# 64 unused bytes behind every operand tile of the fp32r products in a macaron decoder layer

## The chip, the cores and the metric

The kernel runs on one core of one Trainium2 chip. The metric is the device time of one execution in microseconds; the median of three runs of the kernel before is 2115.93 us (2115.43 to 2119.53).

## The reference

One decoder layer on 256 tokens of width 2048, in float32: two SwiGLU feed forwards (width 5632) around a mixer, each behind a norm that a conditioning vector modulates.

```python
mod = (silu(c) @ w_ada + b_ada).reshape(B, 9, D)          # sh, sc, ga of three sublayers
h = rms_norm(x, pre_g) * (1 + sc1) + sh1
x = x + 0.5 * ga1 * rms_norm(swiglu(h, w_gate, w_up, w_down), post_g)
h = rms_norm(x, mix_pre_g) * (1 + sc2) + sh2
x = x + ga2 * rms_norm(hybrid_mixer(h, w_in, w_out, ...), mix_post_g)
h = rms_norm(x, ffn2_pre_g) * (1 + sc3) + sh3
x = x + 0.5 * ga3 * rms_norm(swiglu(h, w_gate2, w_up2, w_down2), post_g2)
```

`swiglu` is `(silu(h @ w_gate) * (h @ w_up)) @ w_down`. The mixer projects h with `w_in`, runs a gated delta rule on eight heads and causal attention on eight, and projects with `w_out`. About 510 MB of weights are read once.

## The kernel before

Each weight is loaded as float32 in pieces of 512 KB (`raw`, line 109) and split into two fp32r parts, `whi` by ScalarE (line 99) and `wlo` by VectorE (line 100). The activations are split in the same way: h into `hh`/`hl`, the product of gate and up into `ghi`/`glo`, the mixer's output into `yth`/`ytl`. A product of two split operands is three matmuls into the same PSUM bank (`prod`, lines 118 to 123): hi by hi, hi by lo, lo by hi.

Three kinds of such products exist. In the feed forwards' gate and up products and in most of the mixer's projections the stationary operand is 128 columns of h and the moving one 512 columns of a weight (1664 triples). In the down products and those with `w_out` the stationary operand is 128 columns of `ghi`/`glo` or `yth`/`ytl`, the moving one again 512 columns of a weight (704 and 128 triples). In the convolved projections (`conv_unit`) the weight is stationary and 256 columns of h move (384 triples). For every matmul TensorE loads 128 new stationary columns (PEld in the profile), and it does so while the matmul before it streams. The order of work is the order of the code; all tiles are placed by pools, tag by tag, and a tag with n buffers has n places.

Where the operand tiles lie follows from their sizes. Every operand tile takes 4096 bytes of a partition, as does `raw`; four places of `raw`, four of `whi`, four of `wlo` and the eight tiles of h stand behind each other, so that all of them have the same offset within 4096 bytes (2496). Behind them stand the small tiles of the pool `sm`, and behind these the places of `ghi`/`glo` or `yth`/`ytl`, each at offset 2560 within 4096 bytes, 64 bytes further than those of h and the weights. The slices that a matmul reads lie at multiples of 512 bytes in their tile. So in every product with h the stationary slice begins at the same offset within 512 bytes as the moving one, and in every product with `ghi`, `glo`, `yth` or `ytl` 64 bytes behind it.

In the list below, a helper of two matmuls for the gates of the mixer (lines 683 and 685) also matters: stationary are 32 or 16 columns of a tile `ab`, moving are 256 columns of h.

Of the kernel before, what the change touches and what calls it, by code (L numbers as in the profile page):

```python
# [17 lines left out]
P = 128  # L18
# [5 lines left out]
PARTS = (range(0, 4), range(4, 8), range(8, NF))  # the blocks of a feed forward's three down products  # L24
# [6 lines left out]
LEAD = 14  # units of the first feed forward that advance together while h comes  # L31
STEPS = ((0, 2), (2, 5), (5, 8), (8, 12), (12, 16))  # the k chunks of h that come together
FIRST = 2  # pieces of w_ada loaded ahead of x
DRAIN, EARLY = 2, 1  # units before a step's end at which its modulation and the next h are made
FILL1, FILL2, FILL3 = 0.52, 0.78, 0.2  # pieces of w_ada per piece of weights
RB, WB = 4, 4
NB4, NB2 = 7, 12
WARM = 18  # products that bridge a norm
APART = 2  # k chunks of a first unit done one token tile at a time
# stages between an instruction on the vector engine and the product that takes its result  # L40
# [35 lines left out]
class Layer:  # L76
# [6 lines left out]
    def step(self):  # L83
        """Moves the work that runs beside the weight products on by one stage."""
        for q in self.queues:
            while q:
                if next(q[0], True):
                    q.pop(0)
                    continue
                break  # L90
# [5 lines left out]
    # ---------------------------------------------------------------- weights  # L96
    def split(self, src, hi, lo):
        """src = hi + lo exactly, in two fp32r parts."""
        self.nc.scalar.copy(hi, src)  # L99
        self.nc.vector.tensor_tensor(lo, src, hi.bitcast(F32), op=ALU.subtract)  # L100

    def wtile(self, src):
        """A [rows, cols] tile of weights, split; returns the parts of its k-th 128 rows."""
        rows, cols = src.shape
        n, h = rows // P, 1024 // cols
        out = []
        for k in range(0, n, h):
            m = min(h, n - k)
            t = self.rawp.tile([P, h, cols], F32, name="raw", tag="raw")[:, :m]
            self.nc.sync.dma_start(t, src[k * P:(k + m) * P].rearrange("(c p) n -> p c n", p=P))  # L110
            hi = self.wp.tile([P, h, cols], F32R, name="whi", tag="whi")[:, :m]
            lo = self.wp.tile([P, h, cols], F32R, name="wlo", tag="wlo")[:, :m]
            self.split(t, hi, lo)
            out.append((hi, lo))
            self.fill()
        return lambda c: (out[c // h][0][:, c % h], out[c // h][1][:, c % h])

    def prod(self, out, a, b, first, last):
        """out += (a0+a1)^T (b0+b1) without a1^T b1, which lies below float32."""
        mm = self.nc.tensor.matmul  # L120
        mm(out, a[0], b[0], start=first, stop=False)  # L121
        mm(out, a[0], b[1], start=False, stop=False)  # L122
        return mm(out, a[1], b[0], start=False, stop=last)  # L123

    def unit(self, acc, rows, src, col, stat, pair=False):
        """acc[tok, 512] = stat^T W[:, col:col+512] over the parts rows of W, four k chunks each.

        With pair, one token tile is done with the last two parts before the other begins them.
        """
        rows = list(rows)  # L130
        groups = [[r] for r in rows[:-2]] + ([rows[-2:]] if pair else [[r] for r in rows[-2:]])
        for g in groups:
            ws = [self.wtile(src[r * 512:(r + 1) * 512, col:col + 512]) for r in g]
            for t in range(NT):
                s = slice(t * P, (t + 1) * P)
                for r, w in zip(g, ws):
                    for c in range(4):
                        hi, lo = stat(r * 4 + c)
                        self.mm = self.prod(acc[t], (hi[:, s], lo[:, s]), w(c), r == rows[0] and c == 0,
                                            r == rows[-1] and c == 3)  # L140
                self.step()

    def bank(self, kind, shape):
        """A PSUM bank for weight products ("acc") or for all else; the tags take turns."""
# [12 lines left out]
    # ---------------------------------------------------------------- modulation  # L157
# [7 lines left out]
    def after(self, eng):  # L165
        """Keeps the first modulation work of an engine behind the norm of the step before."""
# [7 lines left out]
    def ada_step(self, acc, srcs, k):  # L174
        """acc += silu(c)[rows] * rows for the 128-row chunks k.. of some column blocks."""
# [14 lines left out]
    def ada_jobs(self, v, done):  # L190
        """The jobs that stream column block v of w_ada, half a megabyte each."""
# [22 lines left out]
    def fin_shift(self, i, js, acc):  # L214
        """sh of sublayer i for the k chunks js, laid over partitions."""
# [7 lines left out]
    def fin_scale(self, i, js, acc):  # L223
        """g * (1 + sc) of sublayer i."""
# [10 lines left out]
    def fin_gate(self, i, js, acc):  # L235
        """ga * post_g of the mixer, laid over partitions."""
# [9 lines left out]
    def fin_gate_rows(self, i, js, acc):  # L246
        """0.5 * ga * post_g of a feed forward sublayer for the k chunks js, on all partitions."""
# [14 lines left out]
    def gate_rows(self, i, n):  # L262
        """Block n of the gate of sublayer i, on all partitions."""
# [21 lines left out]
    # ---------------------------------------------------------------- norms  # L285
    def rsqrt(self, out, t, tag):
        """out = t ** -0.5 for t > 0: a guess from the bits, then Newton steps to float32.

        With r = a s, a step is s <- (t a^2 s^2 - 3) s and a <- -a / 2; a goes -8, 4, -2, 1.
        """  # L290
# [10 lines left out]
    def rsqrt1(self, out, t, tag):  # L301
        """rsqrt of one value per partition, which can then be a scalar operand.

        With r = a s, a step is s <- (q t s^2 - 3 q / a^2) s and a <- -a^3 / (2 q); a goes 1, -1/2, 1/16, 1.
        """
# [10 lines left out]
    def rstd(self, parts, n, tag):  # L316
        """(sum / n + eps) ** -0.5 from the partial sums parts[P, NT, m]."""
# [7 lines left out]
    def new_h(self):  # L325
        self.hT = [[self.hp.tile([P, 4, SEQ], F32R, name=f"h{p}{g}", tag=f"h{p}{g}") for p in "hl"]
                   for g in range(4)]

    def diag(self, dg, t, s, eng=None):
        """dg[:, t] = diag(s[:, t])."""  # L330
# [4 lines left out]
    def warm(self):  # L335
        """Keeps the tensor engine's clock up while it waits for a norm."""
# [6 lines left out]
    def make_h(self, i, terms, ks, ts=range(NT)):  # L343
        """hT of the k chunks ks; the normalised input is the sum of dg[:, t] src(t, k) over terms,
        or src(t, k) itself.

        Returns the last ScalarE and VectorE instructions.
        """
# [27 lines left out]
    def stats(self):  # L376
        """Partial sums [stat, NT, block] of y^2, 2 x * G y, (G y)^2 and x^2."""
# [8 lines left out]
    def y_block(self, n, t, y, src, st, G, nxt):  # L386
        """y = G * src for block n of one token tile, with its sums."""
# [12 lines left out]
    def finish(self, i, ys, st, first=None):  # L400
        """x += rstd(y) * y; then the next sublayer's h and its first unit, columns col.. of src, or the result."""
# [31 lines left out]
        for t in range(NT):  # L433
# [6 lines left out]
            # mean of (x + r G y)^2  # L440
# [64 lines left out]
    # ---------------------------------------------------------------- feed forward  # L505
    def ffn(self, i, wg, wu, wd, start=None, first=None):
# [5 lines left out]
        def product(u, acc, place=None):  # L512
            """silu(g) * u of a block, in place or in a tile of its own."""
# [10 lines left out]
        def turn(n):  # L524
            """A block of products, transposed and split."""
# [8 lines left out]
            hi = self.gp.tile([P, 4, SEQ], F32R, name="ghi", tag="ghi")  # L534
            lo = self.gp.tile([P, 4, SEQ], F32R, name="glo", tag="glo")
# [43 lines left out]
    def lead(self, units, src, start, product, turn):  # L579
        """The first units, k chunk by k chunk as h comes; all but two gather in SBUF."""  # L580
# [43 lines left out]
    # ---------------------------------------------------------------- mixer  # L624
    def tok_unit(self, col):
        """acc[tok, 512] of w_in's columns col.. ."""
# [4 lines left out]
    def conv_unit(self, which, half):  # L631
        """silu(conv(h W)) of four heads of q, k or v, as [channel, head, tok]."""
# [19 lines left out]
    def norm_sums(self, t, ss):  # L652
        """ss = sums of squares over the channels, [tok, NT, head], plus eps."""
# [13 lines left out]
    def gates(self):  # L667
        """beta, the log decay g and its sums over each chunk."""
# [34 lines left out]
        # softplus(t) = max(t, 0) + log1p(exp(-|t|)), log1p(e) = 2 artanh(e / (2 + e))  # L703
# [26 lines left out]
    def z_unit(self, half, z, acc=None):  # L730
        """z[half] = silu(h W_z) * norm_g."""
# [6 lines left out]
    def gdn(self, half, qT, kT, vT, ssq, ssk, o):  # L738
        """The gated delta rule of four heads, in two chunks of 128 tokens."""
# [46 lines left out]
        for u in range(NT):  # L786
# [4 lines left out]
            # T = ((I + L)^-1)^T by doubling the size of the inverted diagonal blocks  # L791
# [42 lines left out]
        # rms_norm(rq * o) without its gain  # L834
# [19 lines left out]
    def gdn_gate(self, half, o, z):  # L854
        """o * z, transposed and split."""
# [13 lines left out]
    def rope_unit(self, col, name):  # L869
        """Four heads of q or k with the rotary turn, as [channel, head, tok]."""  # L870
# [18 lines left out]
    def moba(self, half, raw, V):  # L889
        """Causal attention inside the one block of 256 tokens."""  # L890
# [66 lines left out]
    def mixer(self, acc):  # L957
        nc = self.nc
        self.yT = [[self.yp.tile([P, 4, SEQ], F32R, name=f"yt{p}{g}") for p in "hl"] for g in range(4)]
# [47 lines left out]
    # ---------------------------------------------------------------- whole layer  # L1007
# [91 lines left out]
    def plan(self, vs, rate):  # L1099
        """Column blocks of w_ada to stream beside the weights, rate pieces per piece."""  # L1100
# [33 lines left out]
```

## Time and profile before

| what | value |
|---|---|
| median of three runs | 2115.93 us |
| span of the profiled execution (its own time is not given beside it) | 2121.1 us |
| TensorE (PE) busy | 2064.7 us, 97% |
| weight loads (PEld) busy | 1724.1 us, 81% |
| VectorE (DVE) busy | 1506.6 us, 71% |
| ScalarE (ACT) busy | 957.4 us, 45% |
| mean DMA rate | 243 GB/s |

The profiled execution's span is 5.2 us above the median of the runs, so it is told of in its own times. In the profile a matmul's duration holds the way through the array, and its end is modelled; matmuls overlap. What a matmul costs TensorE in a row of equal ones is read from the distance between the starts of successive matmuls, which is shorter than the duration of one.

### The profile page before, as it was taken

The numbers are of one execution on the slowest core, as the hardware profiler recorded it, in microseconds if no ns is written. First come the engines' busy times: TensorE is split into PE (matmuls) and PEld (weight loads), VectorE is DVE, ScalarE is ACT, GpSimd is POOL, SyncE is SP. The second block draws the span as 40 slices with busy tenths as digits, with TensorE's granted clock in tenths as the row PEclk, the third lists the DMA queues.
The fourth block names the chain that finished last, engine by engine and source line by source line (L and its number), as shares of the span: only waits on it lengthen the run. The fifth ranks groups of instructions, "written<-read, shape, count | busy, mean of one in ns | idle before, by whom it ended". The sixth has DMA issues, their size and how long they took to land.

```text
span 2121.1 us, 27412 instructions
## 1 busy us (share of the span) xinstructions
PE 2064.7 (97%) x10234; PEld 1724.1 (81%) x10234; DVE 1506.6 (71%) x2001; ACT 957.4 (45%) x1212; POOL 8.5 (0%) x13
## 2 busy tenths in 40 slices
PE   4999999999999999999999999999999999999997
PEld 3777788877888777999988888778887888788886
DVE  6889898767667588897887887785446644545455
ACT  4544354443334356554344364544444444334443
POOL 0000000000000000000000000000000000000001
PEclk9999999999999999999999999999999999999999
DMA  9899987878788786987775777587657866566654
GB/s 309 295 301 308 320 291 244 297 258 311 247 296 290 233 288 188 288 254 232 248 229 181 240 237 267 167 289 241 195 182 254 270 188 190 189 189 188 193 184 138
DMA packets 279509, 514.84 MB, mean 243 GB/s; under 512 B 17536, under 2 KB 79248, under 8 KB 279120
## 3 DMA queue, kind: packets, MB, share of 16 engines
q1 hardware_dynamic: 279088, 512.02, 75.0%
q8 instruction: 80, 1.31, 0.3%
q0 software_dynamic: 288, 1.07, 0.2%
q14 instruction: 53, 0.43, 0.1%
HBM read 510.93 MB, written 2.10 MB: 242 GB/s over the span
## 4 chain that ended last, share of the span: by engine, by line
PE 81%; DMA 9%; DVE 6%; issue 2%; ACT 1%; SPq 1%; DVEq 0%; ACTq 0%
PE acc L121 24%; PE acc L122 24%; PE acc L123 24%; DMA ada<-w_ada 8%; DVE wlo L100 3%; PE ms L755 3%; DVE acc L188 2%; PE ms L207 1%; PE ms L532 1%; DMA G<-gr 1%; PE ms L761 1%; ACT whi L99 0%; DMA raw<-w1g 0%; PE ms L360 0%; PE ms L662 0%
## 5 line engine op out<-in xcount | busy, mean ns | idle before, releaser
L100 DVE TENSOR_TENSOR wlo<-raw,whi 128x1024 fp32r<-128x1024 f32 (+1 forms) x686 | 816.8, 1200 | 409.6 <-ACT whi L99 400.2
L99 ACT CAST whi<-raw 128x1024 fp32r<-128x1024 f32 (+1 forms) x686 | 707.0, 1033 | 880.6 <-PE acc L123 679.6
L121 PE MATMUL acc<-whi,hh 128*128 128x512 f32 x1664 | 661.1, 398 | 6.9 <-DVE part L615 3.8
L122 PE MATMUL acc<-wlo,hh 128*128 128x512 f32 x1664 | 652.8, 393 | 0.9 <-DVE wlo L100 0.8
L123 PE MATMUL acc<-whi,hl 128*128 128x512 f32 x1664 | 650.5, 392 | 0.0
L188 DVE SCALAR_TENSOR_TENSOR acc<-ada,sc,acc 128x1024 f32<-128x1024 f32 (+2 forms) x285 | 349.3, 1226 | 122.4 <-DMA ada<-w_ada 112.9
L121 PEld LDWEIGHTS acc<-whi,hh 128*128 128x128 f32 x1664 | 314.5, 189 | 74.0 <-issue 4.5
L122 PEld LDWEIGHTS acc<-wlo,hh 128*128 128x128 f32 x1664 | 314.5, 189 | 66.0 <-DVE wlo L100 4.0
L123 PEld LDWEIGHTS acc<-whi,hl 128*128 128x128 f32 x1664 | 313.7, 189 | 66.3 <-DVE hl L369 0.5
L121 PE MATMUL acc<-whi,ghi 128*128 128x512 f32 x704 | 280.0, 398 | 0.0
L122 PE MATMUL acc<-wlo,ghi 128*128 128x512 f32 x704 | 278.9, 396 | 0.8 <-DVE wlo L100 0.8
L123 PE MATMUL acc<-whi,glo 128*128 128x512 f32 x704 | 278.2, 395 | 0.0
L122 PEld LDWEIGHTS acc<-wlo,ghi 128*128 128x128 f32 x704 | 132.3, 188 | 33.7 <-DVE wlo L100 1.6
L121 PEld LDWEIGHTS acc<-whi,ghi 128*128 128x128 f32 x704 | 132.2, 188 | 32.3 <-ACT whi L99 0.7
L123 PEld LDWEIGHTS acc<-whi,glo 128*128 128x128 f32 x704 | 132.3, 188 | 31.8
L121 PE MATMUL acc<-hh,whi 128*128 128x256 f32 x384 | 110.9, 289 | 0.0
L123 PE MATMUL acc<-hh,wlo 128*128 128x256 f32 x384 | 108.6, 283 | 0.0
L122 PE MATMUL acc<-hl,whi 128*128 128x256 f32 x384 | 108.6, 283 | 0.0
L122 PEld LDWEIGHTS acc<-hl,whi 128*128 128x128 f32 x384 | 73.7, 192 | 0.0
L121 PEld LDWEIGHTS acc<-hh,whi 128*128 128x128 f32 x384 | 73.6, 192 | 0.1
L123 PEld LDWEIGHTS acc<-hh,wlo 128*128 128x128 f32 x384 | 73.5, 192 | 0.0
L615 DVE TENSOR_TENSOR part<-part,acc 128x512 f32<-128x512 f32 x96 | 65.4, 681 | 4.3 <-PE acc L123 3.5
(283 smaller groups left out, 1316.9 us busy)
## 6 DMA issues: line engine op xcount, KB each, us to landing
ada<-w_ada SPq DMA_DIRECT2D x224, 512.0 KB, 5.7
raw<-w_in SPq DMA_DIRECT2D x112, 512.0 KB, 4.7
raw<-w1d SPq DMA_DIRECT2D x88, 512.0 KB, 5.3
raw<-w2g SPq DMA_DIRECT2D x88, 512.0 KB, 4.5
raw<-w2u SPq DMA_DIRECT2D x88, 512.0 KB, 4.4
raw<-w2d SPq DMA_DIRECT2D x88, 512.0 KB, 4.1
raw<-w1g SPq DMA_DIRECT2D x81, 512.0 KB, 5.1
raw<-w1u SPq DMA_DIRECT2D x81, 512.0 KB, 5.1
```

Of the source, the lines that this page charges most:

```text
L99: self.nc.scalar.copy(hi, src)
L100: self.nc.vector.tensor_tensor(lo, src, hi.bitcast(F32), op=ALU.subtract)
L121: mm(out, a[0], b[0], start=first, stop=False)
L122: mm(out, a[0], b[1], start=False, stop=False)
L123: return mm(out, a[1], b[0], start=False, stop=last)
L188: self.nc.vector.scalar_tensor_tensor(acc, w[:, c], s, acc, op0=ALU.mult, op1=ALU.add)
L207: self.nc.tensor.matmul(ps[:, j:j + 1], acc[:, j * P:(j + 1) * P], self.k("ones")[:, 0:1], start=True, stop=True)
L532: nc.tensor.transpose(ps[:, e, t * P:(t + 1) * P], sl[:, t, c * P:(c + 1) * P], self.k("ident"))
L615: nc.vector.tensor_tensor(pt, pt, acc[t], op=ALU.add)
L755: mm(ps[:, p], lhs(p), rhs(p), start=True, stop=True)
L761: nc.tensor.transpose(ps[:, p], src(p), ident)
```

## The change

A new method `apart` asks the pool for a tile that is 16 elements (64 bytes) longer than the operand and hands out a view of the operand's shape. The operand tiles of the fp32r products, `whi`, `wlo`, the eight tiles of h, `ghi`, `glo` and the eight `yth`/`ytl`, are made by it. Comments and docstrings are dropped besides.

```diff
+APART_BY = 16
+    def apart(self, pool, shape, name, **kw):
+        n = shape[0] * shape[1]
+        return pool.tile([P, n + APART_BY], F32R, name=name, **kw)[:, :n].rearrange("p (a b) -> p a b", a=shape[0])
 def wtile(self, src):
-            hi = self.wp.tile([P, h, cols], F32R, name="whi", tag="whi")[:, :m]
-            lo = self.wp.tile([P, h, cols], F32R, name="wlo", tag="wlo")[:, :m]
+            hi, lo = (self.apart(self.wp, [h, cols], "w" + p, tag="w" + p)[:, :m] for p in ("hi", "lo"))
 def new_h(self):
-        self.hT = [[self.hp.tile([P, 4, SEQ], F32R, name=f"h{p}{g}", tag=f"h{p}{g}") for p in "hl"]
+        self.hT = [[self.apart(self.hp, [4, SEQ], f"h{p}{g}", tag=f"h{p}{g}") for p in "hl"]
 def turn(n):
-            hi = self.gp.tile([P, 4, SEQ], F32R, name="ghi", tag="ghi")
-            lo = self.gp.tile([P, 4, SEQ], F32R, name="glo", tag="glo")
+            hi, lo = (self.apart(self.gp, [4, SEQ], "g" + p, tag="g" + p) for p in ("hi", "lo"))
 def mixer(self, acc):
-        self.yT = [[self.yp.tile([P, 4, SEQ], F32R, name=f"yt{p}{g}") for p in "hl"] for g in range(4)]
+        self.yT = [[self.apart(self.yp, [4, SEQ], f"yt{p}{g}") for p in "hl"] for g in range(4)]
```

The instructions of every engine, their order and their operands are the same before and after; only addresses differ. Offsets within 512 bytes, as the built programs have them:

| tile | before | after |
|---|---|---|
| raw | 448 | 448 |
| whi, its four places | 448 each | 448, 0, 64, 128 |
| wlo, its four places | 448 each | 192, 256, 320, 384 |
| hh of the four groups | 448 each | 448, 64, 192, 320 |
| hl of the four groups | 448 each | 0, 128, 256, 384 |
| ghi, its four places | 0 each | 0, 64, 128, 192 |
| glo, its four places | 0 each | 256, 320, 384, 448 |
| yth of the four groups | 0 each | 0, 128, 256, 384 |
| ytl of the four groups | 0 each | 64, 192, 320, 448 |

From these and the order of the matmuls one can count, for each matmul, how far the stationary slice that is loaded while it streams lies behind its own moving slice, within 512 bytes. Before, the distance is 0 in all but a handful of the matmuls that stream against h or h against a weight, and 64 in those with `ghi`, `glo`, `yth` and `ytl`. After:

| stationary | matmuls | 0 | 64 | 128 | 192 | 256 | 320 | 384 | 448 |
|---|---|---|---|---|---|---|---|---|---|
| h | 5028 | 541 | 230 | 776 | 1022 | 457 | 236 | 798 | 968 |
| ghi, glo | 2111 | 382 | 528 | 385 | 265 | 144 | 4 | 142 | 261 |
| yth, ytl | 384 | 71 | 65 | 49 | 25 | 96 | 30 | 30 | 48 |
| a weight | 1152 | 276 | 60 | 157 | 180 | 11 | 228 | 132 | 108 |

(The row of h holds the 36 matmuls that bridge the norms, line 341, too.)

## Rows read from the trace of the kernel before

**Rows 1.** The page: TensorE's busy time, the chain that ended last.

```profile
PE 2064.7 (97%) x10234; PEld 1724.1 (81%) x10234; DVE 1506.6 (71%) x2001; ACT 957.4 (45%) x1212; POOL 8.5 (0%) x13
PE 81%; DMA 9%; DVE 6%; issue 2%; ACT 1%; SPq 1%; DVEq 0%; ACTq 0%
```

**Rows 2.** Line 121: count, duration ns min/median/max, first and last start, forms.

```profile
L121 PE MATMUL acc<-whi,hh x1664: 387/389/792, 32.5 to 2041.5; 128*128 128x512 f32 x185
...
L121 PE MATMUL acc<-whi,ghi x704: 392/394/801, 363.6 to 2109.6; 128*128 128x512 f32 x176
...
L121 PE MATMUL acc<-hh,whi x384: 277/283/388, 847.0 to 1030.2; 128*128 128x256 f32 x192
...
L121 PE MATMUL acc<-whi,yth x128: 393/394/483, 1256.8 to 1353.0; 128*128 128x512 f32 x128
```

**Rows 3.** Timeline of TensorE, products with h: start us, us, what.

```profile
1449.80 0.39 PE L122 MATMUL acc<-wlo,hh 128*128 128x512 f32 x1
...
1454.33 0.39 PE L121 MATMUL acc<-whi,hh 128*128 128x512 f32 x1
```

**Rows 4.** Timeline of TensorE, down products.

```profile
522.37 0.39 PE L122 MATMUL acc<-wlo,ghi 128*128 128x512 f32 x1
...
527.04 0.39 PE L121 MATMUL acc<-whi,ghi 128*128 128x512 f32 x1
```

**Rows 5.** Timeline of TensorE, convolved projections.

```profile
906.94 0.28 PE L121 MATMUL acc<-hh,whi 128*128 128x256 f32 x1
...
908.98 0.28 PE L123 MATMUL acc<-hh,wlo 128*128 128x256 f32 x1
```

**Rows 6.** Timeline of TensorE behind a long wait, products with h.

```profile
692.00 0.69 PE L532 MATMUL ms<-cst,silu 128*128 128x128 f32 x2 [3.06 <-DVE silu L522]
...
692.92 0.63 PE L122 MATMUL acc<-wlo,hh 128*128 128x512 f32 x1
693.34 0.63 PE L123 MATMUL acc<-whi,hl 128*128 128x512 f32 x1
693.77 0.63 PE L121 MATMUL acc<-whi,hh 128*128 128x512 f32 x1
```

**Rows 7.** Windows, same stretch: PE, PEld, DVE, ACT, POOL busy, PEclk, DMA, GB/s.

```profile
692.20:695.20 3.00, 3.00 (x11) 2.48 (x11) 3.00 (x4) 0.13 (x1) 0.00 (x0) 0.50 1.03 410
699.00:704.00 5.00, 5.00 (x24) 4.14 (x23) 2.45 (x2) 2.11 (x2) 0.00 (x0) 1.00 0.53 159
```

**Rows 8.** Timeline of TensorE behind a short wait, products with h.

```profile
186.48 0.47 PE L121 MATMUL acc<-whi,hh 128*128 128x512 f32 x1 [0.22 <-DVE part L615]
186.79 0.39 PE L122 MATMUL acc<-wlo,hh 128*128 128x512 f32 x1
...
188.87 0.39 PE L121 MATMUL acc<-whi,hh 128*128 128x512 f32 x1
```

**Rows 9.** Timeline of TensorE, stationary operands of 32 and 16 columns.

```profile
852.75 2.03 PE L683 MATMUL ms<-hh,ab 128*32 128x256 f32 x16
854.61 1.99 PE L685 MATMUL ms<-hl,ab 128*16 128x256 f32 x16
856.43 0.28 PE L121 MATMUL acc<-hh,whi 128*128 128x256 f32 x1
```

**Rows 10.** Groups by form, VectorE: the splits of weights.

```profile
L100 DVE TENSOR_TENSOR wlo<-raw,whi 128x1024 fp32r<-128x1024 f32 x658 | 798.4, 1222 | 409.2 <-ACT whi L99 399.8
```

**Rows 11.** Groups by form, ScalarE: the splits of weights.

```profile
L99 ACT CAST whi<-raw 128x1024 fp32r<-128x1024 f32 x658 | 690.8, 1051 | 870.5 <-PE acc L123 679.6 <-PE acc L122 73.2 <-DMA raw<-w1g 31.3
```

**Rows 12.** The longest waits of TensorE: engine line <- releaser, total us, times, longest.

```profile
PE ms L207 <- DVE acc L188: 28.1, 1, 28.1
PE ms L532 <- DVE silu L522: 8.0, 5, 3.1
PE acc L121 <- DVE part L615: 3.8, 5, 2.4
PE acc L121 <- DVE hh L368: 2.0, 2, 1.6
```

## The prediction

> **What bounds the kernel now.** I read first the page: TensorE (PE) is busy for 97% of the span and holds 81% of the chain that ended last; DMA holds 9% and VectorE 6% [rows 1]. The list of its waits is short: apart from the 28.1 us before the first product, the longest sum is 8.0 us in five waits [rows 12]. So the time is the number of matmuls times what each costs TensorE, and where that cost changes, about 81% of it should reach the end; in the rest of the chain a load or a split came last, and a slower TensorE is partly hidden there.
>
> The change leaves every engine's instructions as they are and moves addresses alone. So the next question was whether the trace shows any cost that depends on addresses. The groups by line give the counts (each triple has three matmuls): 3 x 1664 = 4992 matmuls with h stationary, 3 x (704 + 128) = 2496 with `ghi`/`glo` or `yth`/`ytl`, 3 x 384 = 1152 convolved ones [rows 2]. The durations there already differ, 389 ns in the median for h and 394 for the down products [rows 2]. The timeline then gives the cost as the distance of starts:
>
> - h: the 21st start of a steady stretch comes 4.53 us after the first, 226.5 ns each [rows 3].
> - down: 20 steps in 4.67 us, 233.5 ns each [rows 4].
> - convolved, 256 columns: 17 steps in 2.04 us, 120.0 ns each [rows 5].
>
> The two kinds with 512 columns run the same instruction with the same shapes, from the same places of `whi` and `wlo`. What differs is where the stationary slice lies: for h it begins at the offset of the moving slice within 512 bytes, for the down products 64 bytes behind. So there is a cost of 7.0 ns (233.5 - 226.5) that goes with addresses, and it is the pair that already lies apart that pays it.
>
> How large is the whole cost that placing could touch? Behind a wait of 3.06 us the engine ran at granted clock 0.50, which is 1.2 GHz of 2.4 [rows 6, 7], and there the same matmul of h took 430 ns from start to start (693.34 to 693.77), with the timeline's 10 ns step; 512 columns at 1.2 GHz are 426.7 ns. At half the speed nothing is left over. At 2.4 GHz 512 columns are 213.3 ns, so h pays 13.2 ns over its columns, down 20.2 ns, and the convolved ones 13.3 ns over 106.7. The rows with a short stationary operand point the same way: 256 columns with 32 stationary columns take (854.61 - 852.75) / 16 = 116.3 ns, with 16 columns 113.8 ns [rows 9], that is 9.6 and 7.1 ns over the columns. So the extra looks like reads of the next stationary slice that get into the way of the moving stream, more the longer the slice, and partly by where it lies.
>
> One more row: behind a short wait the products with h do not at once take 226.5 ns. From 186.79 to 188.87 there are nine steps, 231.1 ns each [rows 8], and only then the steady pattern. The steady cost of h is thus a favourable pattern that equal matmuls at equal offsets settle into, and 231.1 ns is what the same pair costs while it has not.
>
> **The change part by part.** Weights, h, `ghi`/`glo` and `yth`/`ytl` get places 4160 bytes apart. After that the stationary slice stands at all eight multiples of 64 bytes from the moving one; only 541 of 5028 keep the distance 0 that h has now, and the distances change within a triple (hi to lo moves the weight by 256 bytes) and every second k chunk (next place of the pool). Nothing can settle for long.
>
> Bounds for one matmul of 512 columns, from rows: at best all extra goes, 213.3 ns; a smaller gain is that of the shortest stationary slice, 213.3 + 7.1 = 220.4; at worst of what rows show, all pairs pay as down does, 233.5. I take the unsettled 231.1 ns [rows 8] for all pairs of both kinds: it is the row in which the phase between load and stream varies, as it will after the change, and it lies between the two settled values.
>
> - h: 231.1 - 226.5 = +4.6 ns. Behind each wait some nine matmuls are unsettled already; I count four fifths of 4992 as settled now (an estimate: the waits stand mostly in the first third and around 500 and 700 us). 0.8 x 4992 x 4.6 = +18.4 us.
> - down and output: 231.1 - 233.5 = -2.4 ns, x 2496 = -6.0 us.
> - convolved: no unsettled stretch is shown among the rows; I take the same +4.6 ns, between nothing (120.0 settled) and the 7.0 of the down products: x 1152 = +5.3 us.
> - splits on ScalarE and VectorE: they read `raw` and write `whi`, `wlo`, before all at one offset. 1024 elements take 1051 and 1222 ns [rows 10, 11]. Bounds: if a distance cost as much as it does TensorE (7 in 226, 3%), VectorE would be busy 24 us longer in the kernel, of which its 6% of the chain would show 1.5 us; below nothing, the same. The cover is the engine's idle time: 409.2 us before this group, of which 399.8 ended with ScalarE's cast. I take 0.
> - DMAs: they write `raw`, which stays. 0. The float32 products of the delta rule and the attention: their tiles keep their distances, since all move by the same 1536 bytes. 0.
>
> Sum: 18.4 - 6.0 + 5.3 = +17.7 us of TensorE. Times the 81% of the chain that is TensorE's: +14 us. The profiled span (2121.1) is 5.2 us above the median of the runs, 0.25%, so the sum in its times can be put on the median as it is: 2115.9 + 14 = 2130 us.
>
> Against this stands a rule. The Trainium skill, TensorE: Matmul & The Clock Gate, section What happens when you issue a matmul, says that TensorE has two independent read ports in SBUF, one for the moving operand and one for the weight load, so that loading the next weights takes no bandwidth from the running matmul. By the rule no place of a tile matters and the sum is 0. The trace does not agree: 226.5 and 233.5 ns for the same matmul [rows 3, 4].
>
> **The rivals.**
>
> *Nothing changes* (2116 us, 2112 to 2120). The 7.0 ns would have to come from something other than the distance, say from what the down products' tiles went through, or the gains and losses of the eight distances cancel: with h at +2.0 ns and down at -5 ns the sum is 8.0 - 12.5 + 2.3 = -2 us. For it speaks that only two of eight distances are known, against it that the output projection, at the same distance as the down products in another stage, has the same duration of 394 [rows 2].
>
> *Faster.* The idea of the change: tiles at equal offsets are read in the same part of SBUF at the same time, and other distances than 0 and 64 bytes part the two reads. The place is the weight load beside every streaming matmul; it decides if the six unknown distances cost on average less than about 228.8 ns, since (4992 + 1152) x 2.3 - 2496 x 4.7 is about 2. If every pair came to the 220.4 ns of the shortest slice, h would gain 6.1 x 4992 = 30 us, down 13.1 x 2496 = 33, the convolved ones 6.1 x 1152 = 7; 70 x 0.81 = 57, so 2059 us. A mild form, in which down comes to 226.5 and the rest stays, gains 17.5 x 0.81 = 14: 2102 us. For it speaks that at least 13 ns are there to be won and that half speed shows them gone; against it that the one pair that lies apart costs more than the pair that does not.
>
> *All pairs pay what down pays.* Distance 0 is the one good place, 226.5, and every other costs 233.5. h pays 7.0 x 4992 x 0.89 = 31 us (0.89 is the share that leaves distance 0), convolved 7.0 x 1152 x 0.76 = 6, down gains 7.0 x 0.18 x 2496 = 3: 34 x 0.81 = 28, so 2144 us; if the moving slices' own offsets cost something too, some us more.
>
> **How the numbers follow.** Slower 0.60: the forecast around 2130 with 0.40, and all pairs as down with 0.20. Nothing changes 0.13. Faster 0.27, of which the mild form has 0.15 and the large one 0.12. A difference of 0.2%, 4.2 us, is about what a measurement of this kernel can tell from none. The range from 2092 to 2153 holds the forecast and the worst case with a few us beyond, no change and the mild gain, and leaves out most of the large one; its own range for the forecast alone is 2121 to 2140.
>
> **What would show it.** Counts and order of all groups are unchanged. The median duration of line 121 with h should rise from 389 towards 393, that with `ghi` fall slightly below 394, and the starts in the timeline should no longer repeat at 226.5 but step unevenly between some 224 and 236 ns. In the convolved stretch 120 should become some 123 to 127. The splits should stay at 1051 and 1222 ns. The prediction is wrong if the starts with h come closer than 226 ns (then distance helps), or if they stay at 226.5 at all distances (then the down products' 7 ns had another cause).

## The result and the profile after

The changed kernel takes 2128.19 us in the median (2124.72 to 2132.31, 4 runs), the kernel before 2116.56 us (2115.43 to 2119.53, 4 runs): 11.6 us more. The ratio of the two is 1.0051, with a 95% interval of 1.0030 to 1.0071, so the kernel is slower by half a per cent; 2130 us had been forecast.

The page of the changed kernel, to be held against [rows 1]:

```profile
span 2124.7 us, 27412 instructions
...
PE 2073.7 (98%) x10234; PEld 1720.4 (81%) x10234; DVE 1506.3 (71%) x2001; ACT 955.5 (45%) x1212; POOL 8.5 (0%) x13
...
PE 84%; DMA 7%; DVE 5%; issue 2%; ACT 1%; SPq 0%; DVEq 0%; ACTq 0%
```

Counts are the same, TensorE is busy 9.0 us longer (2073.7 against 2064.7), and its share of the chain that ended last rises from 81% to 84%, while that of the DMAs falls from 9% to 7%: part of the added work seems to stand where a load came last before. The two spans differ by 3.6 us only, since the profiled execution of before lay above its median and this one below. Part of that lies in TensorE's waits and in what it ran at the lower clock: the waits for `silu` fell from 8.0 us [rows 12] to 2.9,

```profile
PE ms L537 <- DVE silu L527: 2.9, 3, 1.6
```

and the matmuls with h that started 415 to 440 ns before the next one, the distance at the lower clock [rows 6, 7], from 32 to 14. How much of this the change did is not shown: in the two executions profiled of e1 and e10 below, which differ in one gap and cost the same per matmul, there were 32 and 23.

The groups of the first product of the triple, now line 126, as in [rows 2] (count, duration ns min/median/max, first and last start, forms):

```profile
L126 PE MATMUL acc<-whi,hh x1664: 387/393/795, 32.0 to 2045.5; 128*128 128x512 f32 x185
...
L126 PE MATMUL acc<-whi,ghi x704: 387/394/792, 363.3 to 2113.2; 128*128 128x512 f32 x176
...
L126 PE MATMUL acc<-hh,whi x384: 274/281/387, 846.8 to 1028.4; 128*128 128x256 f32 x192
```

The median with h went from 389 to 393 ns. The shortest of the down products went from 392 to 387, while their median stayed at 394, and the median of the convolved ones went down, from 283 to 281. The timeline of TensorE gives the distances of starts (start us, us, engine, what): with h, as [rows 3],

```profile
1449.62 0.39 PE L126 MATMUL acc<-whi,hh 128*128 128x512 f32 x1
...
1455.65 0.39 PE L128 MATMUL acc<-whi,hl 128*128 128x512 f32 x1
```

26 steps in 6.03 us, 231.9 ns each where it was 226.5; in the down products, as [rows 4],

```profile
529.69 0.39 PE L127 MATMUL acc<-wlo,ghi 128*128 128x512 f32 x1
...
534.79 0.39 PE L128 MATMUL acc<-whi,glo 128*128 128x512 f32 x1
```

22 steps in 5.10 us, 231.8 ns where it was 233.5; and in the convolved ones, as [rows 5],

```profile
904.80 0.28 PE L127 MATMUL acc<-hl,whi 128*128 128x256 f32 x1
...
907.89 0.28 PE L126 MATMUL acc<-hh,whi 128*128 128x256 f32 x1
```

26 steps in 3.09 us, 118.8 ns where it was 120.0. The splits of the weights did not move, as [rows 10, 11]:

```profile
L101 DVE TENSOR_TENSOR wlo<-raw,whi 128x1024 fp32r<-128x1024 f32 x658 | 798.3, 1222 | 416.5 <-ACT whi L100 414.4
```

```profile
L100 ACT CAST whi<-raw 128x1024 fp32r<-128x1024 f32 x658 | 688.8, 1048 | 886.9 <-PE acc L128 681.4 <-PE acc L127 71.4 <-issue 25.3
```

In what follows the cost of a kind of product is a mean over the whole trace: the distance from the start of each such matmul to the start of TensorE's next one, without those over 262 ns (150 for 256 columns), which hold a wait or the lower clock. About 4800 of the 4992 with h, 2460 of the 2496 down products and 1122 of the 1152 convolved ones are left. All results are in one table. "Down" holds the output projection too. "Distance" says how far the stationary slice that is loaded lies behind the slice that streams, within 256 bytes; the value in brackets is the distance within 512 where it differs. "All four" are the multiples of 64, and a "place" is an offset within 256 bytes. The times of the kernel before moved between 2116.56 and 2118.20 us from one group of runs to the next, so each ratio is to runs of it made beside that kernel's.

| kernel | distance of h | of down | ns h | ns down | ns convolved | time us | ratio to before (95% interval) |
|---|---|---|---|---|---|---|---|
| before | 0 | 64 | 227.6 | 233.3 | 119.8 | 2116.56 | |
| changed | all four | all four | 232.0 | 231.8 | 118.3 | 2128.19 | 1.0051 (1.0030 to 1.0071) |
| e1 | 0 | 0 | 227.6 | 227.1 | 119.8 | 2107.38 | 0.9958 (0.9942 to 0.9973) |
| e2 | 64 | 128 | 233.3 | 232.4 | 117.7 | 2135.19, one run | |
| e3 | 0 (256) | 192 | 227.5 | 229.1 | 119.8 | 2108.75, one run | |
| e4 | 192 (448) | 64 (320) | 229.3 | 233.3 | 116.2 | 2122.27, one run | |
| e5 | all four | all four | 231.6 | 231.8 | 117.6 | 2125.99 | 1.0034 (1.0020 to 1.0047) |
| e6 | all four | all four | 231.8 | 230.6 | 119.0 | 2126.96 | 1.0044 (1.0028 to 1.0059) |
| e7 | 0 (0 and 256) | 64 (64 and 320) | 227.7 | 233.3 | 119.9 | 2117.91 | 1.0002 (0.9989 to 1.0014) |
| e8 | 224 (480) | 32 | 233.3 | 233.3 | 118.4 | 2137.9, one run | |
| e9 | 0, places change | 0, 192, 0 | 231.3 | 232.0 | 117.8 | 2127.99 | 1.0043 (1.0027 to 1.0060) |
| e10 | 0 | 0 (256) | 227.6 | 227.1 | 119.8 | 2107.40 | 0.9948 (0.9935 to 0.9962) |
| e11 | 0, all at place 0 | 0 (256) | 227.6 | 227.0 | 119.8 | 2108.19 | 0.9958 (0.9941 to 0.9974) |

### The profile page after: what moved, and what is told of

Same layout as the page of the kernel before. It is cut to its first block, busy times and chain, and to the rows that moved or that the text cites. A ratio compares the mean times of both kernels' runs of the same rounds, so it can differ in the third digit from the quotient of the medians.

```text
span 2124.7 us, 27412 instructions
## 1 busy us (share of the span) xinstructions
PE 2073.7 (98%) x10234; PEld 1720.4 (81%) x10234; DVE 1506.3 (71%) x2001; ACT 955.5 (45%) x1212; POOL 8.5 (0%) x13
## 4 chain that ended last, share of the span: by engine, by line
PE 84%; DMA 7%; DVE 5%; issue 2%; ACT 1%; SPq 0%; DVEq 0%; ACTq 0%
PE acc L127 26%; PE acc L126 26%; PE acc L128 25%; DMA ada<-w_ada 6%; PE ms L759 3%; DVE wlo L101 2%; DVE acc L193 1%; PE ms L212 1%; PE ms L537 1%; DMA G<-gr 1%; PE ms L765 1%; ACT whi L100 0%; PE ms L365 0%; PE ms L666 0%; DMA raw<-w1u 0%
## 5 line engine op out<-in xcount | busy, mean ns | idle before, releaser
L193 DVE SCALAR_TENSOR_TENSOR acc<-ada,sc,acc 128x1024 f32<-128x1024 f32 (+2 forms) x285 | 349.3, 1226 | 118.8 <-DMA ada<-w_ada 108.9
```

What stands on the lines that cost most here:

```text
L193: self.nc.vector.scalar_tensor_tensor(acc, w[:, c], s, acc, op0=ALU.mult, op1=ALU.add)
```

## The experiments

The first four, and e8, ask what a constant distance costs. They are the kernel before with gaps between pools, which shift all tiles behind them and change no instruction.

**e1, distance 0 for the down products too.**

```diff
-            self.pools(st, {"cp": (1, None), "rawp": (RB, None), "wp": (WB, None),
-                            "hp": (1, None), "sm": (2, None), "psum": (1, PSUM)})
+            self.pools(st, {"cp": (1, None), "rawp": (RB, None), "wp": (WB, None), "hp": (1, None), "sm": (2, None), "gap2": (1, None), "psum": (1, PSUM)})
+            self.gap2.tile([P, 112], F32, name="gap2")
```

The gap holds 112 elements, 448 bytes.

> A gap of 448 bytes ahead of ghi/glo and yth/ytl moves these to the same offset within 512 bytes as the weights: distance 0 everywhere, nothing else changes. Theory (equal pairs at one constant distance settle into a steady pattern; at distance 0 that is 226.7 ns a matmul): the 2496 matmuls with ghi/glo and yth/ytl fall from 233.3 to 226.7 ns, 6.6 x 2496 = 16.5 us less of TensorE, about 14 us off the time: 2102. First rival (each distance has a cost of its own whatever comes before; in the changed kernel distance 0 costs 233): they stay at 233 and the time at 2116. Second rival (the 7 ns of the down products come from something else in that stage): the same, 2116.

The down products fell from 233.3 to 227.1 ns, the time by 9.7 us (2107.38 against 2117.12 for the kernel before, measured beside it). The page's line 121 shows it too, with a median of 389 where [rows 2] have 394:

```profile
L121 PE MATMUL acc<-whi,ghi x704: 387/389/792, 363.0 to 2104.9; 128*128 128x512 f32 x176
```

So what the down products paid beyond h did come from where their tiles lie, and neither from the stage nor from anything done there. This run shows that two of the three theories are wrong; it does not yet show that it is the distance that counts.

**e2, e3, e4, other constant distances.** The same edit with a gap ahead of h's pool (64, 256 and 448 bytes) and one ahead of the down products' tiles (none, 384 and 320 bytes).

> A gap of 64 bytes between the weights' and h's tiles: all products with h at a constant distance of 64 bytes, those with ghi/glo and yth/ytl at a constant 128. Theory: h goes from 226.7 to the 233.3 that the down products had at 64, +33 us of TensorE less what waits hide, about 2143; the down products take some settled value between 226.7 and 233.3. First rival (a cost by distance alone, from the changed kernel's means): h 231.1, down 232.0. Third rival (what counts is the stationary slice's own offset, 0 within 512 bytes being bad): h, now at offset 0, 233, and down, at offset 64, back to 226.7.

> Gaps that put h at a constant distance of 256 bytes and the down products at 192. Theory: both settle; the values are not known, between 226.7 and 233.4 each (the span of the two known ones). If reads meet in parts of SBUF that repeat every 256 bytes, h stays at 226.7; if they repeat every 512, it goes to 233. First rival (cost by distance alone): h 233.1, down 230.8, spread over 226 to 238 and not settled.

> Gaps that put h at a constant distance of 448 bytes (64 ahead of the moving slice) and the down products at 320. Theory: both settle at values between 226.7 and 233.4. First rival (cost by distance alone): h 231.3, down 230.9, not settled. The convolved products have the distance 64 here (the weight is stationary): 120 if 256 columns do not mind, 123 to 127 if they pay as the down products do.

Line 121 of e2 shows h where the down products had been [rows 2],

```profile
L121 PE MATMUL acc<-whi,hh x1664: 388/394/796, 32.5 to 2054.0; 128*128 128x512 f32 x185
```

and so does its timeline:

```profile
1450.76 0.39 PE L122 MATMUL acc<-wlo,hh 128*128 128x512 f32 x1
...
1454.96 0.39 PE L122 MATMUL acc<-wlo,hh 128*128 128x512 f32 x1
```

These are 18 steps in 4.20 us, 233.3 ns each, so at a distance of 64 h costs what the down products did. The values at 0 and 256 are the same (227.6, 227.5), those at 64 and 320 (233.3, 233.3), and 192 and 448 (229.1, 229.3); 128 costs 232.4. So with one constant distance the cost repeats every 256 bytes in the three pairs that were tried, and 0 is the best of the four multiples of 64. The rival with the changed kernel's means (231.1 at 64 for h) misses by 2 ns. For the convolved products, where the weight is stationary and 256 columns move, it is the other way: distance 0 is the dearest that was tried (119.8), 64 the best (116.2 in e4).

**e5 and e6, one part of the change alone.** e5 keeps `apart` for the weights, e6 for h, `ghi`/`glo` and `yth`/`ytl`.

```diff
 # e5, against the changed kernel
-        self.hT = [[self.apart(self.hp, [4, SEQ], f"h{p}{g}", tag=f"h{p}{g}") for p in "hl"]
+        self.hT = [[self.hp.tile([P, 4, SEQ], F32R, name=f"h{p}{g}", tag=f"h{p}{g}") for p in "hl"]
 # ... and the same for gp and yp
 # e6, against the changed kernel
-            hi, lo = (self.apart(self.wp, [h, cols], "w" + p, tag="w" + p)[:, :m] for p in ("hi", "lo"))
+            hi, lo = (self.wp.tile([P, h, cols], F32R, name="w" + p, tag="w" + p)[:, :m] for p in ("hi", "lo"))
```

> Only whi and wlo get the 64 bytes; h, ghi/glo and yth/ytl stand as before. The distance then changes with the place of the pool, every second k chunk (six matmuls), through 0, 64, 128, 192 within 256 in equal shares for all kinds. Theory A (a matmul's cost goes with its distance within 256 bytes, as the kernels with one constant distance have it: 227 at 0, 233.3 at 64, 232.4 at 128, 229.2 at 192): the mean is 230.5 for h and for the down products, convolved about 118; 2.9 x 4992 - 2.8 x 2496 - 1.5 x 1152 = +5.8 us of TensorE, about 2121. Theory B (beyond that, a change of distance leaves the pair unsettled, as behind a wait): h and down at 232, as in the changed kernel, +17 us of TensorE, about 2130.

> Only h, ghi/glo and yth/ytl get the 64 bytes; whi and wlo stand as before. The distance then changes within each triple (hi to lo, 64 bytes) and with each group of h: 0 and 128 a third each, 64 and 192 a sixth each. Theory A (cost by distance within 256): h (227 + 232.4) / 3 + (233.3 + 229.2) / 6 = 230.2, down about 230.4: +13 - 7 - 1 = +5 us of TensorE, about 2121. Theory B (changes unsettle): since the distance changes at every second or third matmul, h and down at 232 or above, about 2130.

Either part alone costs nearly what both do: 1.0034 and 1.0044. The times, 2126.0 and 2127.0, lie between A's 2121 and B's 2130. h stands at 231.6 and 231.8, above the 230.5 and 230.2 of the sum over distances, near the 232 of theory B; down stands at 231.8 in e5 (B's value) and at 230.6 in e6 (A's is 230.4). So theory A alone does not hold. In e6 the weights stand at one place, and from 360 us on the trace has the matmuls in the order of the code, so that each one's distance is known: h costs 231.5 ns at 0, 229.3 at 64, 233.3 at 128 and 231.1 at 192. Distance 0 is not the cheap one there, and 64 is not the dear one. The same reading of the changed kernel had given 233 at 0 and 231.1 at 64 (the expectations of e1 and e2).

**e7, other unused bytes.**

```diff
-            hi = self.wp.tile([P, h, cols], F32R, name="whi", tag="whi")[:, :m]
+            hi = self.wp.tile([P, 1024 + 64], F32R, name="whi", tag="whi")[:, :1024].rearrange("p (a b) -> p a b", a=h)[:, :m]
```

> Only whi gets unused bytes, 256 instead of 64. The distances of h change between 0 and 256 within 512 bytes with each place of the pool and between hi and lo; within 256 bytes they are all 0, those of the down products all 64. Theory A and a repeat of 256 bytes: h stays at 227.5, down at 233.3, the time at 2117. If any change of place unsettles the pair (theory B in its plain form), or if the repeat is 512: h at 230 or more, +12 us or more.

Nothing moved: 227.7, 233.3, 119.9 ns and a ratio of 1.0002. The line with h has the median of [rows 2]:

```profile
L121 PE MATMUL acc<-whi,hh x1664: 387/389/792, 32.2 to 2041.3; 128*128 128x512 f32 x185
```

Tiles with 256 unused bytes between them are as good as tiles with none, so the size of the gap is what harms, not that there is one.

**e8, between the multiples of 64.** Gap of 480 bytes ahead of h, none ahead of the down products.

> Gaps that put h at a constant distance of 480 bytes (32 ahead of the moving slice), the down products at 32 behind, the convolved ones at 32 behind. Theory A says nothing of distances between multiples of 64; if the cost goes evenly between its neighbours, h lies at 228.3 (between 229.2 and 227.4) and down at 230 (between 227.1 and 233.3), convolved at 118 (between 119.8 and 116.1). A value below 226.7 for h would show a better place than any so far.

Both expected values for 512 columns are missed: 233.3 ns at 32 bytes ahead and at 32 behind, so the cost does not go evenly between its neighbours. The good place is narrow: 32 bytes to either side the whole 6 ns are lost. The convolved products, at 118.4, are near the expected 118.

**e9, equal distances at changing places.** `wlo` gets a pool of its own 64 bytes on, h's hi tiles stand before its lo tiles with 64 bytes between, and gaps of 192 and 128 bytes bring h and the down products' tiles to the place of `whi`.

```diff
+            self.gap0.tile([P, 16], F32, name="gap0")
+            self.gap1.tile([P, 48], F32, name="gap1")
+            self.gap2.tile([P, 32], F32, name="gap2")
 # ... the gaps stand between wp and wq, ahead of hp, and ahead of the stages' pools
-            lo = self.wp.tile([P, h, cols], F32R, name="wlo", tag="wlo")[:, :m]
+            lo = self.wq.tile([P, h, cols], F32R, name="wlo", tag="wlo")[:, :m]
 # ... in new_h
+            m = n + (16 if (p, g) == ("h", 3) else 0)
 # ... all hi tiles of h before the lo tiles
+        self.hT = list(zip(*[[tile(p, g) for g in range(4)] for p in "hl"]))
```

> wlo and hl stand 64 bytes apart (within 256) from whi and hh, so that every load for h keeps the distance 0 from the slice that streams, while the places of successive matmuls change by 64 bytes twice in each triple. ghi, glo, yth and ytl stand at one place, so that the down products have the distances 0, 192, 0 within each triple. Theory A (cost by distance alone): h stays at 227.5 ns, convolved at 119.8, down goes to (2 x 227 + 229.2) / 3 = 227.8; the time at 2108. Theory B (a change of distance adds to it): h 227.5, down about 230 to 231, the time 2111 to 2113. Theory C (a change of the places themselves adds to it): h at 230 to 232 too, the time above 2118.

h lies at 231.3 ns and the time at 2128 us, as theory C has it; A and B had 227.5 for h. The timeline of e9 with h:

```profile
1449.68 0.39 PE L122 MATMUL acc<-wlo,hh 128*128 128x512 f32 x1
...
1454.77 0.39 PE L123 MATMUL acc<-whi,hl 128*128 128x512 f32 x1
```

22 steps in 5.09 us, 231.4 ns, though every slice that is loaded has the distance 0 from the slice that streams. The steps do repeat: among the second matmuls of the triple 788 of 1636 take 232 ns, among the third 997 take 229; but they repeat at a higher cost. The products with `ghi` and `glo`, with distances of 0 and 192, do not profit from them either (232.0). One could also count a matmul's distance to the stationary slice that it is multiplied with, which is 0, 192 and 64 in the triple of h. That does not explain the cost: the three take 232.1, 231.3 and 230.5 ns, where constant distances of 0, 192 and 64 cost 227.6, 229.3 and 233.3. What the good kernels have in common is therefore more than a distance: all slices that TensorE reads one after the other in a stretch, stationary and moving, begin at one and the same place within 256 bytes. Whether it is the change of the moving slice's place or of the stationary one's that costs is not shown, as both change in e9.

**e10 and e11, the best version.** One gap of 192 bytes ahead of the down products' tiles (e10), and with 64 bytes more ahead of `raw` (e11), which moves all operand tiles from place 192 to place 0.

```diff
 # e10 and e11, ahead of the stages' pools
+            self.gap2.tile([P, 48], F32, name="gap2")
 # e11 alone, ahead of rawp
+            self.gap0.tile([P, 16], F32, name="gap0")
```

> The kernel before with one gap of 192 bytes ahead of ghi/glo and yth/ytl, so that these lie 256 bytes behind the moving slice. Theory A with the repeat of 256 bytes: the same as the gap of 448, 227 ns for the down products and about 2107 to 2108. If 512 bytes counted instead, the down products would lie between 229 and 233 and the time above 2111.

> A gap of 64 bytes ahead of raw and one of 192 ahead of ghi/glo and yth/ytl: all operand tiles, and raw, begin at offset 0 within 256 bytes, where the kernel with the gap of 192 alone has them all at 192. If only the equality of the places counts: h 227.6, down 227, convolved 119.8 ns, the time 2107. If the place itself counts (offset 0 was where the slow stationary slices of the down products stood): 229 to 233 ns, the time above 2115.

The down products of e10 in the timeline:

```profile
518.69 0.39 PE L123 MATMUL acc<-whi,glo 128*128 128x512 f32 x1
...
523.45 0.39 PE L123 MATMUL acc<-whi,glo 128*128 128x512 f32 x1
```

21 steps in 4.76 us, 226.7 ns, where [rows 4] show 233.5. And the page:

```profile
span 2107.3 us, 27412 instructions
...
PE 2048.0 (97%) x10234; PEld 1721.1 (82%) x10234; DVE 1505.4 (71%) x2001; ACT 958.7 (45%) x1212; POOL 8.5 (0%) x13
...
PE 79%; DMA 9%; DVE 7%; issue 2%; ACT 1%; SPq 1%; DVEq 0%; ACTq 0%
```

TensorE is busy 16.7 us less than in [rows 1]. The time is 2107.40 us, a ratio of 0.9948 (0.9935 to 0.9962): faster than the kernel before and, by 20.8 us of medians, than the changed one. e11 gives the same in ns and in time, so of the two places tried neither is better; what matters is that it is one.

## Why the prediction was right, step by step

*TensorE's cost per matmul sets the time, addresses alone change it.* Right. Counts, splits and DMAs stayed. Kernels that differ by one gap of 192 bytes differ by 9.6 us (e10 against 2117.01). The Trainium skill, TensorE: Matmul & The Clock Gate, section What happens when you issue a matmul, has it that loading the next weights takes no bandwidth from the running matmul, since TensorE has two independent read ports. The trace disagrees as far as it shows that the places of the two operands matter by up to 6 ns in 227; where in the engine or the memory the two meet, no run here shows.

*h loses.* Right. The term was +18.4 us; by the means it is (232.0 - 227.6) x 4820 = +21 us. I had taken the cost at 231.1, the row behind a wait [rows 8]; it came out at 232.0.

*Down gains a little.* Right in its sign. The term was -6.0 us; it is (231.8 - 233.3) x 2457 = -3.7 us. (In the table of distances ahead of the prediction the row of `yth`, `ytl` adds up to 414 for 384 matmuls; no term rests on it.)

*Convolved loses.* This step failed, in its sign: +5.3 us was forecast, (118.3 - 119.8) x 1123 = -1.7 us came. I had carried the cost of 512 moving columns over to 256, without a row for it; e2 and e4 show that there distance 0 is the dearest of those tried, 119.8 against 117.7 and 116.2. In the sum the 7.0 us that this step was out by were made up for in part by h and the down products, whose terms came out 2.8 and 2.3 us higher than forecast; that is luck.

*The sum* is 21 - 3.7 - 1.7 = +15.6 us of TensorE where 17.7 had been counted, and 11.6 us of it reach the end, 74% where I took 81%. In e10 it is (6.3 x 2079 + 5.9 x 374) = 15.3 us of which 9.6 arrive, 63%; in e9 about 12 of which 11.0 arrive. The share of the chain is thus a rough guide to what arrives, not a factor. In the two profiles shown above less arrives than in the medians, 3.6 us: the matmuls with h that the means leave out fell from 205, with 82.1 us from start to start, to 168 with 61.2.

*Nothing can settle.* Right for the change, but the picture behind it was half of the matter. Products with h are sorted here by how many of their kind have followed each other since a wait or other work. Before, the first five steps take 230.9 ns in the mean, the next five 228.7 and all later ones 226.8; the down products of e10 take 230.9, 228.2 and 226.7. So there is a cost into which matmuls with equal places settle, as [rows 8] had it. Where places change the fall is missing: the changed kernel has 232.1, 233.1 and 231.9 for h, e9 has 231.4, 230.9 and 231.3. What the prediction lacked is that a constant distance alone is not enough. The down products of the kernel before, at 64, take 233.3, 233.4 and 233.3, more than the unsettled cost of h, and distance 0, by which I had sorted the pairs, is no help when the places change from one matmul to the next (e9).

*The rivals.* "Nothing changes" is out by the interval. "Faster" is out too: different places, its means, are what costs. Its mild form, in which the down products come to 226.5, was reached with equal places instead, at 2107.4 us (e10) where 2102 had been counted, and no arrangement tried took more of the 13 ns over the columns than the 6 that the down products lost there. "All pairs pay what down pays" is e8's case for 512 columns, 2137.9 us in one run, and not that of the change.

Open: why the cost repeats every 256 bytes, why equal places settle, and why 256 moving columns prefer another distance. No kernel tried put the convolved products at distance 64 with the others at 0; by e4's 116.2 ns that would be 3.6 x 1123 = 4 us of TensorE (an estimate).

## What to carry to other kernels

Before spreading tiles over different offsets, measure from the starts of successive matmuls what the present offsets cost: here, with 512 moving columns, the equal ones were the cheap ones, and one gap that made all operands equal within 256 bytes was worth 0.5%, while gaps that made them different cost 0.5%. Where a kernel streams full-speed fp32r products with a new stationary slice for each, print the offsets of all operand tiles and look for two kinds of product with the same shape and different cost. A cost read for one shape is not that of another: with half the moving columns, and the weight as the stationary operand, the order of the distances turned round.

## What the hardware showed that was not expected

- The cost of a 512-column fp32r matmul with a new stationary slice repeats with the distance of the two operands every 256 bytes: 227.6 ns at 0, 233.3 at 32, 64 and 224, 232.4 at 128, 229.1 and 229.3 at 192, each with all moving slices at one place.
- With 256 moving columns and the weight stationary the order differs: 119.8 ns at 0, 118.4 at 32, 116.2 at 64, 117.7 at 192.
- Equal distances do not do it alone: 231.3 ns at distance 0 when the places of successive matmuls differ by 64 bytes (e9).
- With equal places the cost falls over the first ten matmuls behind a wait or other work, from 230.9 to 226.8 ns (h, kernel before).
- VectorE and ScalarE, which read and write the same tiles, did not notice: 1222 and 1048 to 1051 ns for 1024 elements before and after.
